# A two-layer conformer and sparse-attention stack: the layers' convolution in two stages, with the blocks' inputs made first and each block's sum over the taps a block later

## The chip, the cores and the metric

The kernel runs on one core of a Trainium2 chip. The metric is the device time of one execution in microseconds (us), the median of several runs. The engines are called as in the profile: PE (TensorE's matmuls) and PEld (its weight loads), DVE (VectorE), ACT (ScalarE), POOL (GpSimd) and SP (SyncE, which here only issues transfers). ACTq and SPq are the DMA issues of ACT and SP.

## The reference, cut to what matters

The program is a block of mixer, cross attention and mixture of experts, and then `second_block`, two layers of a convolution branch beside an attention branch. Only the layers are touched.

```python
for l in range(DEPTH_2):                       # 2 layers, x is 512 positions x 1024
    p = h @ w_in[l]                            # h: normalized, modulated x
    u_val, u_gate, g_conv, c_q, c_kv, k_idx, w_idx, g_attn = jnp.split(p, offsets, axis=-1)
    y_conv = conformer_conv(u_val, u_gate, ...) * jax.nn.silu(g_conv)
    y_attn = dsa_attention(c_q, c_kv, k_idx, w_idx, ...) * jax.nn.silu(g_attn)
    y = jnp.concatenate([y_conv, y_attn], axis=-1) @ w_out[l]
    x = x + gate[:, None, :] * rmsnorm(y, g_post[l])

def conformer_conv(u_val, u_gate, conv_w, conv_b, ln_g, ln_b, w_pw2):
    a = u_val * jax.nn.sigmoid(u_gate)
    y = <causal depthwise convolution of a, 31 taps, 512 channels> + conv_b
    return jax.nn.silu(layernorm(y, ln_g, ln_b)) @ w_pw2

def dsa_attention(...):
    score = jnp.einsum("bth,bths->bts", w_b, jax.nn.relu(s_raw))   # 8 index heads
    _, sel = lax.top_k(score, k_top)           # the 128 best keys of each query
    ...                                        # softmax attention over those keys, 8 heads
```

## The kernel before, in words

Values are kept as pairs of f16 (a high and a low part), so that each product is three matmuls (`mm3`: wh by hh, wh by hl, wl by hh). `mm` (L98, L99) records every matmul, so all PE rows have line 99 and are told apart by their tiles. `split` makes a pair: ACT writes the high part (L119), DVE the low part (L120). `load_w` does that for a block of weights: an SP transfer to `raw` (two buffers), then two halves of `wh` by ACT and of `wl` by DVE; four pairs of weights have buffers. `proj_feat` is the product of one block of weights, 256 columns in two halves, with the layer's input X (`hh`, `hl`): 24 matmuls of 128x512 for 128 features.

The order in which each engine takes its instructions is set by a scheduler at build time; `high_priority` moves instructions ahead and `after(x)` orders them behind x. In a layer the parts that matter here stand in this order in the code:

- `select` for query blocks 1, 2 and 3: for each of 8 index heads, PE makes scores (`at<-idx`, two banks of PSUM), ACT takes the positive part (`re`, L1583), DVE adds it into `sc` (L1586 for the first head, L1588 for the others). Then 16 rounds of MAX (L1592) and MATCH_REPLACE (L1593) on DVE take out the 128 best scores, and `msk` (L1595) marks them.
- `conv`, called twice for two blocks of 128 channels: the gate's projection into bank `cv`, a tanh on ACT (`cth`, L1650), the value's projection into a bank `mm`, the gating on DVE (L1653), the split into `cu` (L119, L120), and four DMAs issued by ACT (L1663) that copy `cu` into `R`, each with four shifted copies of 32 channels in 128 partitions. POOL builds the diagonal weights `wd` (L1669). Then 96 matmuls `po<-R,wd` sum over the taps (8 shifts by 3 parts by 4 groups) into the one bank `po`, and ACT moves it out with the bias (`cacc`, L1678). `R`, `cu` and `wd` have two buffers each.
- `conv_norm`: the layernorm; its mean is four f32 products `cv<-cacc,ones`, one for each block.
- twice: `gates` of the attention (projection into `cv`, ACT `gth` L1337, DVE `ga` L1339), two times `dsa` (two heads each: query projection `mm<-cq,uq`, scores `at<-kv,q` with the mask added by `at<-msk,identb`, softmax, transposes `tr`, value products `po<-pT,v`), then the convolution's gates and `conv_out`.
- `out_gain` builds the row `G` for the output: two ACT DMAs `gt<-in_r` (L1309), each followed by a POOL operation on `G` (L1310). `gt` shares its two buffers with `wd`.

The two lines that the split replaces in `layer` are

```python
for k in range(2):
    self.conv(pool, l, X, sp, cw, acc, k)
```

Of the kernel before, what the change touches and what calls it, by code (L numbers as in the profile page):

```python
# [12 lines left out]
F16 = mybir.dt.float16  # L13
BF16 = mybir.dt.bfloat16
I32 = mybir.dt.int32
AF = mybir.ActivationFunctionType
OP = mybir.AluOpType
# [3 lines left out]
P = 128  # L21
# [29 lines left out]
SA = 16.0  # L51
SW = 256.0
SX = 4.0
INV = 1.0 / (SA * SW)
# [9 lines left out]
class Kern:  # L64
# [43 lines left out]

    def mm3(self, out, L, R, start, stop):
        self.mm(out, L[0], R[0], start, False)  # L110
        self.mm(out, L[0], R[1], False, False)
        return self.mm(out, L[1], R[0], False, stop)

# [692 lines left out]
    def route_tile(self, low, pool, i, hf):  # L806
# [45 lines left out]

        R = sm("R8", NE)
        nc.vector.max(m8, LM)
        top = self.top[:, i]
        nc.vector.tensor_copy(top[:, 0:2], m8[:, 0:2])
        nc.vector.match_replace(R, top, LM, 3.0e38)
        Mh = self.Mh[:, i]
# [590 lines left out]
    def layer(self, pool, l, xin, follow):  # L1449
        nc, a = self.nc, self.a  # L1450
        sp, (X, cq, kv, widx, filled) = self.sp[l], xin[0]
        big = a["w2_big"]
# [36 lines left out]
        v = self.u8(pool, "v2").rearrange("p (h i f) -> p h i f", h=2, i=NT)  # L1489
# [6 lines left out]
        cw = pool.tile([P, 2, S], F16, name="cw2", tag="h", bufs=BUFS["h"])  # L1496
        self.split(sp[:, 24:152], cw[:, 0, :P], cw[:, 1, :P], SW)
        acc = pool.tile([P, 4, S], F32, name="cacc", tag="cacc", bufs=1)
        for k in range(2):
            self.conv(pool, l, X, sp, cw, acc, k)  # L1500
        z = self.conv_norm(pool, sp, acc)
        yh, yl = (pool.tile([P, 4, 1084], F16, name=n, tag="Y", bufs=2).rearrange("p g m -> p (g m)")[:, :DC * S]
                  .rearrange("p (c t) -> p c t", c=DC) for n in ("y2h", "y2l"))
# [3 lines left out]
            self.split(raw.rearrange("p (c f) -> p c f", c=4), wp[:, 0], wp[:, 1], SW)  # L1507
        wp = wp[:, 0], wp[:, 1]
        for k in range(2):
            gas = self.gates(pool, big[l, 8 + k], X)  # L1510
            for b in range(2):
                done = self.dsa(pool, gas[b], uq, cqh, cql, kvh, kvl, v[:, 0], v[:, 1], msk, yh, yl, 2 * k + b)
            gcs = self.gates(pool, big[l, 6 + k], X)
            for b in range(2):
                self.conv_out(pool, wp, z, gcs[b], 2 * k + b, yh, yl)

        G = self.out_gain(pool, l)
        ws = []
# [22 lines left out]
        for i in range(NT):  # L1541
            y = pool.tile([P, D], F32, name="yo", tag="yo", bufs=2)
            ss = pool.tile([P, 2], F32, name="oss", tag="oss", bufs=4)
            for hf in range(2):
                o = slice(hf * 512, (hf + 1) * 512)
                po = self.bank("mm")
# [13 lines left out]
            for hf in range(2):  # L1560
                o = slice(hf * S, (hf + 1) * S)
                nc.vector.scalar_tensor_tensor(self.x[i][:, o], y[:, o], r[:, 1:2], self.x[i][:, o],
                                               op0=OP.mult, op1=OP.add)
# [76 lines left out]
        nc.vector.tensor_tensor(ga, po, ga, OP.mult)  # L1640
        return self.split(ga, yh[:, 4 + hp], yl[:, 4 + hp], 0.5 * INV / 1024.0)

    def conv(self, pool, l, X, sp, cw, acc, k):

        nc, big = self.nc, self.a["w2_big"]
        wv, wg = self.load_w(big[l, 2 + k]), self.load_w(big[l, 4 + k])
        for b in range(2 * k, 2 * k + 2):
            pg = self.proj_feat(wg, X, 256, b % 2, out=self.bank("cv"))
            th = self.t2(pool, "cth", "v")
            nc.scalar.activation(th, pg, AF.Tanh, scale=0.5 * INV)  # L1650
            pu = self.proj_feat(wv, X, 256, b % 2)
            with self.tc.high_priority():
                nc.vector.scalar_tensor_tensor(th, th, 1.0, pu, op0=OP.add, op1=OP.mult)  # L1653

            u = pool.tile([P, 2, 544], F16, name="cu", tag="cu", bufs=2)
            nc.gpsimd.memset(u[:, :, 0:30], 0.0)
            nc.gpsimd.memset(u[:, :, 542:544], 0.0)
            with self.tc.high_priority():
                self.split(th, u[:, 0, 30:542], u[:, 1, 30:542], 0.5 * SA * INV)
            R = pool.tile([P, 4, 1084], F16, name="R", tag="Y", bufs=2)  # L1660
            for g in range(4):
                ug = u[32 * g:32 * g + 32]
                nc.scalar.dma_start(R[:, g], bass.AP(tensor=ug.tensor, offset=ug.offset,  # L1663
                                                   ap=[list(ug.ap[0]), [1, 4], [1, 1084]]))

            wd = pool.tile([P, 2, 32, 32], F16, name="wd", tag="yo", bufs=2)
            with self.after(self.lat_pow):
                for h in range(2):
                    nc.gpsimd.tensor_tensor(wd[:, h], self.mask4[:, None, :].to_broadcast([P, 32, 32]),  # L1669
                                            cw[:, h, 32 * b:32 * b + 32, None].to_broadcast([P, 32, 32]), OP.mult)  # L1670
            py = self.bank("po")
            for q in range(8):
                for n, (x, y) in enumerate(((0, 0), (0, 1), (1, 0))):
                    for g in range(4):
                        o = y * 544 + 4 * q
                        self.mm(py[32 * g:32 * g + 32], wd[:, x, 8 * g + q], R[:, g, o:o + S],
                                q + n == 0, q == 7 and n == 2)
            nc.scalar.activation(acc[:, b], py, AF.Identity, scale=INV, bias=sp[:, 152 + b:153 + b])  # L1678

    def conv_norm(self, pool, sp, acc):  # L1680

# [231 lines left out]
```

## Time and profile before

| | before |
|---|---|
| median of 3 runs | 1646.88 us (1646.11 to 1650.43) |
| the profiled execution, and its span | 1654.38 us, 1652.7 us |
| PE busy | 1511.4 us (91% of the span) |
| DVE busy | 973.2 us (59%) |
| ACT busy | 592.0 us (36%) |
| POOL busy | 113.7 us (7%) |

The span is cut from the first to the last recorded instruction of one profiled execution; the busy times are sums over it. PE is the engine with the most work, but the shares are means over stages with different limits.

### The profile page before, as it was taken

To read this page: it belongs to the slowest core of one execution; us is meant where nothing else is said; L and a number is where in the kernel's file an instruction comes from. 1 tells how busy PE (TensorE), PEld (TensorE's weight loads), DVE (VectorE), ACT (ScalarE), POOL (GpSimd) and SP (SyncE) were. 2 spreads that over 40 slices of the span, in tenths; PEclk is the share of its full clock that TensorE was granted. 3 is DMA by queue.
4 is the path that set the end of the run, shared out by engine and by line. 5 is a ranking of instruction groups with operands and counts; after the bars stand their busy time and mean duration, and the time that the engine had idled before them with its cause. 6 is when DMAs were issued, how large, how long until landed. Compare 5 with 4: busy or idle time off the path is not lost.

```text
span 1652.7 us, 25283 instructions
## 1 busy us (share of the span) xinstructions
PE 1511.4 (91%) x10208; PEld 828.4 (50%) x10208; DVE 973.2 (59%) x2076; ACT 592.0 (36%) x1230; POOL 113.7 (7%) x124
## 2 busy tenths in 40 slices
PE   7999999879996999999999987988999989888998
PEld 5344586765583444444444435323444863334457
DVE  5778848877754324233242447886746568947552
ACT  5355545423531101111011126522737454227461
POOL 0210001000000000000000021212000020110000
PEclk9999899999998999999999998989999999989999
DMA  8410223788457999999999940334011223230201
GB/s 284 157 62 12 91 82 111 290 255 328 147 224 283 385 426 427 427 426 427 426 426 426 426 154 14 109 105 131 10 68 43 75 96 100 67 121 26 77 26 52
DMA packets 55609, 323.03 MB, mean 195 GB/s; under 512 B 8720, under 2 KB 11584, under 8 KB 19520
## 3 DMA queue, kind: packets, MB, share of 16 engines
q1 hardware_dynamic: 45136, 306.01, 47.6%
q10 hardware_dynamic: 10352, 15.37, 3.5%
q8 instruction: 81, 1.33, 0.3%
q14 instruction: 40, 0.33, 0.1%
HBM read 310.35 MB, written 3.69 MB: 190 GB/s over the span
## 4 chain that ended last, share of the span: by engine, by line
PE 48%; DVE 9%; DMA 3%; ACT 3%; issue 2%; POOL 1%; ACTq 0%; DVEq 0%; POOLq 0%
PE h L99 12%; PE y L99 6%; PE mm L99 6%; PE cv L99 6%; PE po L99 4%; PE tr L99 4%; PE at L99 3%; PE ga L99 3%; DMA R<-cu 3%; DVE sc L1593 1%; DVE m L1592 1%; PE tr L1634 1%; DVE wl L120 1%; PE tr L103 1%; DVE sc L1588 1%
## 5 line engine op out<-in xcount | busy, mean ns | idle before, releaser
L99 PE MATMUL h<-raw,xg 128*64 128x512 f32 x1024 | 223.0, 593 | 0.0
L120 DVE SCALAR_TENSOR_TENSOR wl<-raw,wh 128x1024 f16<-128x1024 f32 (+1 forms) x107 | 133.3, 1251 | 63.6 <-ACT wh L119 63.0
L99 PEld LDWEIGHTS <-wh 128*128 128x128 f16 x1104 | 107.7, 100 | 124.2 <-issue 32.7
L99 PEld LDWEIGHTS h<-raw,xg 128*64 128x64 f32 x1024 | 73.5, 137 | 146.1 <-issue 145.7
L119 ACT ACTIVATE wh<-raw 128x1024 f16<-128x1024 f32 (+1 forms) x107 | 110.6, 1042 | 94.2 <-PE mm L99 43.4
L958 DVE SCALAR_TENSOR_TENSOR hm<-hm,h 128x512 f32<-128x512 f32 x16 | 11.0, 687 | 180.5 <-ACT hm L957 180.5
L99 PE MATMUL y<-raw,hT 128*64 128x512 f32 x512 | 113.6, 595 | 0.0
L987 DVE SCALAR_TENSOR_TENSOR x<-tr,x 128x512 f32<-128x512 f32 x128 | 86.4, 687 | 12.3 <-PE tr L99 10.3
L99 PEld LDWEIGHTS <-wl 128*128 128x128 f16 x552 | 54.9, 99 | 63.9 <-issue 14.4
L957 ACT ACTIVATE hm<-h 128x512 f32<-128x512 f32 x16 | 9.6, 597 | 207.2 <-PE h L99 182.8
L99 PEld LDWEIGHTS <-hh 128*128 128x128 f16 x768 | 74.7, 101 | 17.8 <-issue 3.7
L99 PE MATMUL po<-R,wd 128*32 128x512 f16 x768 | 56.9, 401 | 23.8 <-DMA R<-cu 23.8
L120 DVE SCALAR_TENSOR_TENSOR yl<-y,cw,yh 128x512 f16<-128x512 f32 x32 | 24.0, 750 | 89.1 <-ACT yh L119 89.1
L99 PE MATMUL cv<-hh,wh 128*128 128x512 f16 x192 | 74.8, 390 | 0.0
L99 PE MATMUL cv<-hl,wh 128*128 128x512 f16 x192 | 74.7, 389 | 0.0
L99 PE MATMUL cv<-hh,wl 128*128 128x512 f16 x192 | 74.7, 389 | 0.0
L99 PEld LDWEIGHTS <-hl 128*128 128x128 f16 x640 | 64.2, 100 | 14.0 <-issue 2.1
L99 PEld LDWEIGHTS y<-raw,hT 128*64 128x64 f32 x512 | 35.3, 137 | 70.3 <-issue 69.0
L99 PE MATMUL ga<-Sel,hl 128*128 128x128 f16 x480 | 67.8, 223 | 0.0
L99 PE MATMUL ga<-Sel,hh 128*128 128x128 f16 x480 | 67.8, 223 | 0.0
L1250 DVE CUSTOM_DVE_ANT_0 raw<-raw,cact 128x1024 f32<-128x1024 f32 x48 | 58.3, 1236 | 13.4 <-DMA raw<-in_w_ada 12.3
L119 ACT ACTIVATE yh<-y,cw 128x512 f16<-128x512 f32 x32 | 22.0, 687 | 114.2 <-PE y L99 112.9
(429 smaller groups left out, 3487.0 us busy)
## 6 DMA issues: line engine op xcount, KB each, us to landing
raw<-in_w_moe SPq DMA_DIRECT2D x192, 1024.0 KB, 12.1
raw<-in_w_pre SPq DMA_DIRECT2D x34, 1024.0 KB, 5.3
raw<-in_w_big SPq DMA_DIRECT2D x30, 1024.0 KB, 4.9
raw<-in_w_ada SPq DMA_DIRECT2D x24, 1024.0 KB, 6.6
R<-cu ACTq DMA_DIRECT2D x32, 271.0 KB, 5.2
x<-in_x_tm SPq DMA_DIRECT2D x4, 512.0 KB, 7.3
gt<-in_r ACTq DMA_DIRECT2D x4, 512.0 KB, 5.2
out<-x SPq DMA_DIRECT2D x4, 512.0 KB, 2.6
```

The source lines that it names most:

```text
L99: self.last_mm = self.pin(self.nc.tensor.matmul(out, lhsT, rhs, start=start, stop=stop, skip_group_check=True))
L103: return self.pin(self.nc.tensor.transpose(out, src, ident))
L119: return (nc.scalar.activation(hi, src, func, scale=scale), nc.vector.scalar_tensor_tensor(lo, src, scale, hi, op0=OP.mult, op1=OP.subtract))
L120: nc.vector.scalar_tensor_tensor(lo, src, scale, hi, op0=OP.mult, op1=OP.subtract))
L957: nc.scalar.activation(hm[:n], ph[0][:n], AF.Tanh, scale=0.5 / SA)
L958: nc.vector.scalar_tensor_tensor(hm[:n], hm[:n], 1.0, ph[0][:n], op0=OP.add, op1=OP.mult)
L987: self.last_add = nc.vector.scalar_tensor_tensor(xo, pc, 1.0 / 1024.0, xo, op0=OP.mult, op1=OP.add)
L1250: nc.vector.tensor_tensor_reduce(w, w, cact, 1.0, 0.0, OP.mult, OP.add, to)
L1588: nc.vector.scalar_tensor_tensor(sc, re[:, :W], s, sc, op0=OP.mult, op1=OP.add)
L1592: nc.vector.max(m8, sc)
L1593: nc.vector.match_replace(sc, m8, sc, -3.0e38)
L1634: nc.tensor.transpose(pt[:, (i - k) * P:(i - k + 1) * P], ps_[i][:, k * P:(k + 1) * P], self.ident)
```

## The change

`conv` becomes two functions. `conv_in` makes a block's input (projections, gating, split, the four shifted copies), and issues the copies alternately on ACT's and SP's queue. `conv_sum` builds `wd` and sums over the taps, its matmuls ordered behind the last matmul recorded before. The order is: inputs 0 and 1, the second pair of weights, sum 0, input 2, sum 1, input 3, the first `gates` of the attention (moved here from below the layernorm), sum 2, sum 3. Nothing is computed that was not computed before.

```diff
@@ layer
-        for k in range(2):
-            self.conv(pool, l, X, sp, cw, acc, k)
+        ws = [[self.load_w(big[l, n]) for n in (2, 4)]]
+        Rs = [self.conv_in(pool, X, *ws[0], b) for b in (0, 1)]
+        ws.append([self.load_w(big[l, n]) for n in (3, 5)])
+        gas = None
+        for b in range(4):
+            self.conv_sum(pool, sp, cw, acc, Rs[b], b)
+            if b < 2:
+                Rs.append(self.conv_in(pool, X, *ws[1], 2 + b))
+            if b == 1:
+                gas = self.gates(pool, big[l, 8], X)
...
         for k in range(2):
-            gas = self.gates(pool, big[l, 8 + k], X)
+            gas = gas or self.gates(pool, big[l, 8 + k], X)
...
-            gcs = self.gates(pool, big[l, 6 + k], X)
+            gas, gcs = None, self.gates(pool, big[l, 6 + k], X)
@@ conv_in
+            for g in range(4):
+                ug = u[32 * g:32 * g + 32]
+                (nc.scalar, nc.sync)[g % 2].dma_start(R[:, g], bass.AP(tensor=ug.tensor, offset=ug.offset,
+                                                                       ap=[list(ug.ap[0]), [1, 4], [1, 1084]]))
+        return R
@@ conv_sum
+        wd = pool.tile([P, 2, 32, 32], F16, name="wd", tag="yo", bufs=2)
+        with self.after(self.lat_pow):
+            ...
+        py = self.bank("po")
+        with self.after(self.last_mm):
+            for q in range(8):
+                ...
+        nc.scalar.activation(acc[:, b], py, AF.Identity, scale=INV, bias=sp[:, 152 + b:153 + b])
```

On PE, at the first sum of layer 0, the order before puts the first tap matmuls singly between matmuls of the next block's projection; each waits for one of the four copies (the DMAHW semaphores):

```order
L99 MATMUL cv<-hl_9249,wh 128x512
L99 LDWEIGHTS wd [waits Pool_49]
L99 MATMUL po<-R,wd 32x512 [waits DMAHW7_49]
L99 LDWEIGHTS wl
L99 MATMUL cv<-hh_9248,wl 128x512
L99 LDWEIGHTS wh
L99 MATMUL mm<-hh_9248,wh 128x512
```

In the order of the changed kernel both blocks' projections stand ahead, and the 96 matmuls follow each other:

```order
L99 MATMUL mm<-hl_9249,wh 128x512
L99 LDWEIGHTS wl
L99 MATMUL mm<-hh_9248,wl 128x512
L99 LDWEIGHTS wd [waits Pool_49]
L99 MATMUL po<-R,wd 32x512 [waits DMAHW7_49]
L99 LDWEIGHTS wd
L99 MATMUL po<-R,wd 32x512 [waits DMAHW0_49]
L99 LDWEIGHTS wd
L99 MATMUL po<-R,wd 32x512 [waits DMAHW1_49]
```

So the single tap matmuls and what stood between them have changed places: 48 matmuls of block 1's input now lie between the end of block 0's input and the first tap matmul. Sums 1, 2 and 3 stand whole in the same way; behind input 3 come the 24 matmuls of the first gate, 7 of the query projection, the 24 of the second gate, sum 2, and sum 3 one f32 product later.

On DVE, at the end of the rounds for query block 3 of layer 0 (`sc_10057`), the order before has block 3's gating behind the mask, and no gate:

```order
L1592 MAX m_10115<-sc_10057 128x8 [waits DVE_49]
L1593 MATCH_REPLACE sc_10057<-m_10115,sc_10057 128x512 [waits DVE_49]
L1595 TENSOR_SCALAR msk_10148<-sc_10057 128x512 [waits DVE_49]
L1653 SCALAR_TENSOR_TENSOR cth<-cth,mm 128x512 [waits PE_49]
L120 SCALAR_TENSOR_TENSOR cu<-cth,cu 128x512 [waits DMAHW4_49,DMAHW7_49,DMAHW0_49,Activation_49]
L120 SCALAR_TENSOR_TENSOR wl<-raw,wh 128x1024 [waits Activation_49]
```

In the order of the changed kernel (line numbers there are 7 or 8 higher) the gating, two halves of weights and the first gate stand among the last rounds:

```order
L1660 SCALAR_TENSOR_TENSOR cth<-cth,mm 128x512 [waits PE_49,Activation_49]
L1601 MATCH_REPLACE sc_10057<-m_10115,sc_10057 128x512 [waits DVE_49]
L1600 MAX m_10115<-sc_10057 128x8 [waits DVE_49]
L120 SCALAR_TENSOR_TENSOR cu<-cth,cu 128x512 [waits DMAHW6_49,DMAHW5_49,DMAHW7_49,DMAHW0_49,Activation_49]
L1601 MATCH_REPLACE sc_10057<-m_10115,sc_10057 128x512 [waits DVE_49]
L120 SCALAR_TENSOR_TENSOR wl<-raw,wh 128x1024 [waits DMAHW5_49,Activation_49]
L1600 MAX m_10115<-sc_10057 128x8 [waits DVE_49]
L120 SCALAR_TENSOR_TENSOR wl<-raw,wh 128x1024 [waits Activation_49]
L1339 SCALAR_TENSOR_TENSOR ga<-gth,cv 128x512 [waits Activation_49]
```

The first gate `ga` reads bank `cv`; the second gate's first matmul (`cv<-hh`, which waits for DVE) needs that bank, there is only one, and sums 2 and 3 stand behind it on PE. Between the last score addition and `ga` stand 14 and a half rounds, two `cth`, two `cu` and four `wl`.

On ACT, before, the move of sum 2 and the two `gt` transfers stand apart, with block 3's copies and two query splits between them:

```order
L1678 ACTIVATE cacc<-po,sp_3445 128x512 [waits PE_49]
L1309 DMA gt<-in_r 128x1024 [waits Pool_49]
L119 ACTIVATE cu<-cth 128x512 [waits DMAHW7_49,DMAHW0_49,DVE_49]
L119 ACTIVATE wh<-raw 128x1024 [waits PE_49]
L1663 DMA R<-cu 128x1x1084 [waits DVE_49,Pool_49]
L1663 DMA R<-cu 128x1x1084
L1663 DMA R<-cu 128x1x1084 [waits DMAHW2_49]
L119 ACTIVATE q_11022<-mm 128x512 [waits PE_49]
L1663 DMA R<-cu 128x1x1084 [waits DMAHW3_49]
L119 ACTIVATE q_11107<-mm 128x512 [waits PE_49]
L1309 DMA gt<-in_r 128x1024 [waits DMAHW6_49,DMAHW4_49,Pool_49]
```

The changed kernel has them together, the second gate's tanh ahead and the move of sum 3 right behind:

```order
L1337 ACTIVATE gth<-cv 128x512 [waits PE_49]
L1689 ACTIVATE cacc<-po,sp_3445 128x512 [waits PE_49]
L1309 DMA gt<-in_r 128x1024 [waits DMAHW4_49]
L1309 DMA gt<-in_r 128x1024 [waits DMAHW4_49,Pool_49]
L1689 ACTIVATE cacc<-po,sp_3445 128x512 [waits PE_49]
```

The second `gt` waits for POOL's addition of the first, so `cacc` of sum 3 now queues behind that transfer and that addition.

## Rows read from the trace of the kernel before

**Rows 1.** The page's chain of work that ended last, by line.

```profile
PE h L99 12%; PE y L99 6%; PE mm L99 6%; PE cv L99 6%; PE po L99 4%; PE tr L99 4%; PE at L99 3%; PE ga L99 3%; DMA R<-cu 3%; DVE sc L1593 1%; DVE m L1592 1%; PE tr L1634 1%; DVE wl L120 1%; PE tr L103 1%; DVE sc L1588 1%
```

**Rows 2.** Windows: stretch, us, busy PE PEld DVE ACT POOL, PEclk, DMA share, GB/s.

```profile
1065.80:1160.50 94.70, 81.67 (x599) 31.68 (x598) 70.32 (x163) 21.56 (x33) 13.97 (x14) 0.91 0.36 103
1160.50:1300.00 139.50, 134.35 (x773) 73.73 (x773) 86.36 (x186) 86.23 (x190) 2.10 (x3) 0.98 0.17 57
1386.60:1482.50 95.90, 79.62 (x599) 31.62 (x598) 70.21 (x162) 21.57 (x33) 13.48 (x10) 0.91 0.35 102
1482.50:1602.00 119.50, 114.81 (x599) 56.87 (x599) 72.20 (x161) 75.16 (x168) 1.02 (x1) 0.97 0.11 37
```

**Rows 3.** PE's waits, 1036 to 1245, then 1350 to 1600: total, times, longest.

```profile
PE po L99 <- DMA R<-cu: 10.2, 6, 3.0
...
PE po L99 <- DMA R<-cu: 13.6, 8, 3.0
```

**Rows 4.** PE's timeline in both layers' convolution: start, us, instruction [idle before].

```profile
1065.79 0.38 PE L99 MATMUL mm<-hh,wh 128*128 128x512 f16 x1
1070.97 0.38 PE L99 MATMUL cv<-hh,wh 128*128 128x512 f16 x1
1078.16 0.38 PE L99 MATMUL po<-R,wd 128*32 128x512 f16 x1 [2.06 <-DMA R<-cu]
1134.10 5.36 PE L99 MATMUL po<-R,wd 128*32 128x512 f16 x93
1140.69 2.74 PE L99 MATMUL cv<-cacc,ones 128*128 128x512 f32 x6
1147.65 0.38 PE L99 MATMUL at<-kv,q 128*128 128x128 f16 x3
1160.47 0.39 PE L99 MATMUL at<-msk,identb 128*128 128x512 bf16 x1
1482.47 0.39 PE L99 MATMUL at<-msk,identb 128*128 128x512 bf16 x1
```

**Rows 5.** DVE's waits, 1065.8 to 1122, then 1386.6 to 1442.

```profile
DVE sc L1588 <- ACT re L1583: 3.8, 2, 3.3
DVE wl L120 <- ACT wh L119: 3.0, 1, 3.0
...
DVE sc L1588 <- ACT re L1583: 2.9, 2, 2.4
DVE wl L120 <- ACT wh L119: 1.7, 1, 1.7
```

**Rows 6.** DVE's timeline, first and last score addition and first rounds of block 3.

```profile
1092.91 1.59 DVE L1586 TENSOR_SCALAR sc<-re,widx 128x512 f32<-128x512 f32 x1
1108.64 0.75 DVE L1588 SCALAR_TENSOR_TENSOR sc<-re,widx,sc 128x512 f32<-128x512 f32 x1 [3.26 <-ACT re L1583]
1109.90 0.69 DVE L1592 MAX8 m<-sc 128x8 f32<-128x512 f32 x1
1111.41 0.69 DVE L1592 MAX8 m<-sc 128x8 f32<-128x512 f32 x1
...
1413.72 0.46 DVE L1586 TENSOR_SCALAR sc<-re,widx 128x512 f32<-128x512 f32 x1
1427.40 0.75 DVE L1588 SCALAR_TENSOR_TENSOR sc<-re,widx,sc 128x512 f32<-128x512 f32 x1 [0.56 <-ACT re L1583]
```

**Rows 7.** DVE's weight splits, by line, 1065.8 to 1160.5: busy, mean ns, idle before.

```profile
L120 DVE SCALAR_TENSOR_TENSOR wl<-raw,wh 128x1024 f16<-128x1024 f32 x8 | 9.7, 1215 | 3.2 <-ACT wh L119 3.2
```

**Rows 8.** POOL's timeline: building a block's weights, adding to G.

```profile
1090.40 3.81 POOL L1669 TENSOR_TENSOR wd<-mask,cw 128x1024 f16<-128x1024 f16 x2 [7.96 <-PE po L99]
1143.34 3.31 POOL L1310 TENSOR_TENSOR G<-G,gt 128x1024 f32<-128x1024 f32 x1 [10.01 <-DMA gt<-in_r]
```

**Rows 9.** Time to landing of gt (1100 to 1500) and of raw (1340 to 1500).

```profile
DMA to landing us min/median/max: 3.7/5.2/8.2
...
DMA to landing us min/median/max: 4.8/5.0/9.6
```

More of the change, by code (lines that the diff above doesn't have):

```diff
@@ L1641, in dsa, with conv_in @@
         return self.split(ga, yh[:, 4 + hp], yl[:, 4 + hp], 0.5 * INV / 1024.0)
[L1643 to L1660, printed above, removed]
+    def conv_in(self, pool, X, wv, wg, b):
+        nc = self.nc
+        pg = self.proj_feat(wg, X, 256, b % 2, out=self.bank("cv"))
+        th = self.t2(pool, "cth", "v")
+        nc.scalar.activation(th, pg, AF.Tanh, scale=0.5 * INV)
+        pu = self.proj_feat(wv, X, 256, b % 2)
+        with self.tc.high_priority():
+            nc.vector.scalar_tensor_tensor(th, th, 1.0, pu, op0=OP.add, op1=OP.mult)
+        u = pool.tile([P, 2, 544], F16, name="cu", tag="cu", bufs=2)
+        nc.gpsimd.memset(u[:, :, 0:30], 0.0)
+        nc.gpsimd.memset(u[:, :, 542:544], 0.0)
+        R = pool.tile([P, 4, 1084], F16, name="R", tag="Y", bufs=2)
+        with self.tc.high_priority():
+            self.split(th, u[:, 0, 30:542], u[:, 1, 30:542], 0.5 * SA * INV)
@@ L1661, in conv @@
             for g in range(4):
                 ug = u[32 * g:32 * g + 32]
[L1663 to L1670, printed above, removed]
@@ L1671, in conv, with conv_sum @@
-            py = self.bank("po")
+                (nc.scalar, nc.sync)[g % 2].dma_start(R[:, g], bass.AP(tensor=ug.tensor, offset=ug.offset,
+                                                                       ap=[list(ug.ap[0]), [1, 4], [1, 1084]]))
+        return R
+    def conv_sum(self, pool, sp, cw, acc, R, b):
+        nc = self.nc
+        wd = pool.tile([P, 2, 32, 32], F16, name="wd", tag="yo", bufs=2)
+        with self.after(self.lat_pow):
+            for h in range(2):
+                nc.gpsimd.tensor_tensor(wd[:, h], self.mask4[:, None, :].to_broadcast([P, 32, 32]),
+                                        cw[:, h, 32 * b:32 * b + 32, None].to_broadcast([P, 32, 32]), OP.mult)
+        py = self.bank("po")
+        with self.after(self.last_mm):
@@ L1677, in conv @@
                                 q + n == 0, q == 7 and n == 2)
-            nc.scalar.activation(acc[:, b], py, AF.Identity, scale=INV, bias=sp[:, 152 + b:153 + b])
+        nc.scalar.activation(acc[:, b], py, AF.Identity, scale=INV, bias=sp[:, 152 + b:153 + b])
     def conv_norm(self, pool, sp, acc):
```

## The prediction

> **What bounds the kernel now.** I read the page's chain first: nearly all of it is PE, but one transfer stands on it, the copies `R<-cu`, with 3% of the span [rows 1]. The windows say where PE is not full. In the convolution of layer 0, 1065.8 to 1160.5, PE is busy 81.67 of 94.7 us, in layer 1 79.62 of 95.9; in the attention behind it 134.35 of 139.5 and 114.81 of 119.5 [rows 2]. So some 29 us are idle in the two stretches that the change rewrites, and the attention behind is bound by PE's work, with gaps of about 5 us in each layer. PE's waits name most of the idle time: the first tap matmuls wait for the copies, 10.2 us in layer 0 and 13.6 in layer 1 [rows 3]. Third I read DVE, which does the selection's rounds at the same time and works 70 of those 95 us [rows 2]: it is the engine that PE will wait for next.
>
> **The change part by part.** *The copies.* Before, block 0's input ends at 1070.97 and its first tap matmul waits at 1078.16; between them lies as much projection as the scheduler found [rows 4]. A projection of 24 matmuls takes 1070.97 − 1065.79 = 5.18 us, 0.216 each [rows 4]. After, 48 of them, 10.4 us, lie between block 0's input and its sum. That covers what lay between the end of the input and the first tap matmul before, 7.2 us, with 3.2 us to spare for the other three copies, and two queues issue two each. Blocks 1 to 3 have more work between. So I take the 23.8 us of waits for copies [rows 3] as gone. They don't enter the sum as such: what remains is to see what PE meets instead. For that I follow DVE.
>
> *DVE up to the first gate.* `gates` is moved ahead of sum 2, and its second half needs bank `cv`, which is free only after DVE's `ga` of the first half. On DVE `ga` stands behind 14 and a half rounds of block 3's selection. So PE's sum 2 now depends on when that selection started. Before, the last score addition of block 3 begins at 1108.64 in layer 0 and 1427.40 in layer 1 [rows 6]. Ahead of it DVE works the same instructions in both orders (two `cth`, two `cu`, four `wl` and the rounds of blocks 1 and 2). Its waits there are for `re` and for `wh`: 3.8 + 3.0 = 6.8 us in layer 0, 2.9 + 1.7 = 4.6 in layer 1 [rows 5]. I read both as PE or ACT being held behind the copies, and take them as gone: 1101.8 and 1422.8 (if they stay, 1108.6 and 1427.4, and that much of the gain goes). From there to the end of `ga`: 1.26 to the first round (1109.90 − 1108.64), 14 rounds of 1.51 (1111.41 − 1109.90) = 21.1, half a round 0.7 [rows 6], two `cth` and two `cu` 2.7 and `ga` 0.7 (0.7 each, a little under the 0.75 of the addition, the same kind on as much), four `wl` at 1.215 = 4.9 [rows 7]: 31.4. So `ga` ends at 1133.2 and 1454.2.
>
> *PE up to there.* PE is held at the fifth index score until about 1094, since that bank waits for DVE's first addition (1092.91 before, [rows 6]). Then: 33 matmuls of input 2, 7.1; four scores of three matmuls, 2.6; sum 1, 5.4 (5.36 for 93 [rows 4]); input 3, 10.4; the first gate, 5.2; six query matmuls, 1.3; and 2 for a stretch at half clock (the granted clock of the window is 0.91 [rows 2]). That is 34, PE is at the bank at about 1128, and waits 5 us. This is the new wait.
>
> *PE from there.* The second gate 5.2, with 1.7 for half clock after the wait; sum 2, 5.5; one f32 product of `cacc` 0.9 (2.74 for three, which the row counts as six [rows 4]); sum 3, 5.5: 18.8. Sum 3 ends at 1152.0 and 1473.0. Before, the row behind it starts at 1160.47 and 1482.47 [rows 4]: earlier by 8.5 and 9.5.
>
> *What PE has done by then.* More by the two gates, 48 × 0.216 = 10.4 us. Less by five or six query matmuls 1.1, two f32 products 1.8, and the first head's scores up to the last mask, 4480 columns at 0.216 us for 512, 1.9. Net 5.6 us more work done. The lead is 8.5 + 5.6 = 14.1 in layer 0, 15.1 in layer 1, together 29.2.
>
> *What is given back.* On ACT `cacc` of sum 3 queues behind the second `gt`, which waits for the first `gt` and POOL's addition. The first is issued when sum 2 ends, 1145.7; landing 5.2 [rows 9] and addition 3.3 [rows 8] give 1154.2, then `cacc` 0.8: 1155.0. PE has 1.8 us of other f32 products behind 1152.0, so it waits 1.2. By the landings of 3.7 and 8.2 [rows 9] it is 0 to 4.2. And the gates were cover in the attention: 10.4 us of PE work that could lie in any gap there no longer does. The gaps of the attention are 5.2 and 4.7 us [rows 2] with the cover; without it they could grow by 0 to 10.4 per layer. I take 1.5, near the low end, since other work of the same kind (the convolution's gates, `conv_out`, the second gates) stays there. Given back: 2 × (1.2 + 1.5) = 5.4.
>
> *Taken at nothing:* two of each block's four copies stand on SP's queue between weight transfers (`raw`), and a copy that waits there for its `cu` holds the transfers behind it. They land in 4.8 to 9.6 us [rows 9], and PE's other projections cover that as long as one block's (10.4 us) lies between; the price if not is rival B's. POOL builds the same `wd`, under PE's projections.
>
> *The sum.* −29.2 + 5.4 = −23.8 us. Profiled execution: 1654.4 → 1630.6. The runs' median is 7.5 us below that execution, so 1646.9 → **1623**.
>
> *A rule against the rows.* POOL's build of `wd` (1090.40, 3.81 us [rows 8]) lay under DVE's first addition of block 3, which took 1.59 us at 1092.91; in layer 1 the same instruction, without it, took 0.46 [rows 6]. The Trainium skill, page "SBUF — State Buffer", section "Who interferes with whom", says that DVE and GpSimd share a port pair, held by one for a whole instruction while the other is fully blocked. The row agrees in sign, not in size (1.1 us more, not the whole of POOL's instruction). In the new order `wd` is built earlier, right behind sum 0; by the rule DVE would be 1.1 us earlier per layer and the sum −26, about 1621. It is left out of the sum.
>
> **The rivals.** *B, a shallower gain.* The gates' weights now come in the middle of the convolution. If their `raw` lands in 9.6 us instead of 5.0, or the attention's cover is worth half of the 10.4, 5 us per layer go: −14, **1633**. For it: copies stand between weight transfers on SP's queue. Against it: the median landing is 5.0. *C, the full gain.* All of the 23.8 us of waits for copies and the half clock (0.09 of 95 us, 8.5 per layer [rows 2]) come back, with no new wait on `ga`: −41, **1606**. Against it: DVE works 70 of 95 us and its rounds can't be earlier than their scores. *D, no change.* All of the lead is given back in the attention, **1647**: it needs gaps there to grow by 15 us in each layer, more than the cover removed. *E, slower.* The first head's scores start at 1147.65 before [rows 4]; after, they stand behind sum 3 and three f32 products, at about 1155.9. If the attention ends by its own chain (scores, softmax, transposes, split, value product) and not by PE's work, each layer ends 8.2 us later: +16, **1663**. It decides from the point where PE's gaps in the attention exceed what it did ahead; against it, PE is busy 134.35 of 139.5 us there [rows 2].
>
> **How the numbers follow.** Mine 0.55, its own range 1614 to 1632 (the `gt` wait 0 to 4.2, the lost cover 0 to 5, the DVE waits gone wholly or half). B 0.20, C 0.12, D 0.05, E 0.08. The range for 8 in 10 takes in my case, B and the way down to C: 1606 to 1637. A change under 0.3%, about 5 us, could hardly be told from none: faster 0.87 (mine, B, C), same 0.05, slower 0.08.
>
> **What would show it.** Right: no waits of `po` for `R`; the rows of tap matmuls are 96 long; a wait of `cv` for DVE's `ga` of about 5 us per layer; a wait of `cv<-cacc` for ACT of 1 us; sum 3 ends some 9 us earlier in its layer. Wrong: a wait for `R` at sum 0 (10.4 us too little), a wait on `ga` well over 5 (then DVE's waits did not go), or an attention window with over 8 us of gaps.

## The result, and the profile after

The changed kernel takes 1629.53 us (median of 4 runs, 1626.61 to 1635.61) against 1648.5 for the kernel before (4 runs): a ratio of 0.9882, interval 0.986 to 0.9904, 19 us less. A second timing of the same file gave 1624.22 against 1650.27, 0.9846 (0.9829 to 0.9863). The profiled execution has a span of 1628.6 us, 24.1 less than the one of before; 3.1 of these lie ahead of the first layer's convolution, in code that did not change (the first index score starts at 1037.66 instead of 1040.78), so 21.0 belong to the layers: 4.7 in layer 0 and 16.3 in layer 1, where 11.4 and 12.4 were forecast.

PE's waits, layer 0 (1036 to 1245) and then layer 1 (1350 to 1600): total, times, longest. They answer to [rows 3]; only the lines that bear on the two stages are shown.

```profile
PE cv L99 <- DVE ga L1339: 6.0, 3, 4.5
PE at L99 <- ACT re L1591: 2.2, 1, 2.2
PE cv L99 <- ACT csq L1704: 2.1, 1, 2.1
PE po L99 <- DMA R<-cu: 0.8, 1, 0.8
...
PE cv L99 <- DVE ga L1339: 3.7, 2, 3.3
PE at L99 <- ACT re L1591: 3.6, 2, 3.1
PE cv L99 <- ACT cacc L1689: 1.6, 1, 1.6
```

The waits of the tap matmuls for their copies have gone from 10.2 + 13.6 to 0.8 us. In their place stand the wait of bank `cv` for DVE's gate, 4.5 and 3.3 us, and behind sum 3 a wait for `csq` (the squares of the layernorm) in layer 0 and for `cacc` in layer 1.

The page's chain by line no longer lists `R<-cu`, which stood there with 3% [rows 1]; the one transfer in the list is one of weights:

```profile
PE h L99 13%; PE y L99 7%; PE mm L99 6%; PE cv L99 5%; PE tr L99 4%; PE at L99 3%; PE ga L99 3%; PE po L99 3%; DVE sc L1601 2%; DVE m L1600 2%; DVE wl L120 2%; DMA raw<-in_w_big 2%; PE tr L1642 1%; PE tr L103 1%; DVE sc L1596 1%
```

Windows of the convolution and of the attention (columns as in [rows 2]), layer 0 and layer 1; each convolution starts as in [rows 2], earlier by what its layer begins earlier (3.1 and 7.8 us):

```profile
1062.70:1153.60 90.90, 82.30 (x628) 34.36 (x626) 71.86 (x165) 22.13 (x30) 11.57 (x13) 0.92 0.41 113
1153.60:1262.20 108.60, 104.79 (x540) 54.53 (x537) 65.17 (x159) 69.49 (x165) 3.38 (x2) 0.94 0.10 35
1378.80:1466.00 87.20, 80.83 (x623) 33.67 (x621) 69.38 (x159) 22.07 (x30) 7.91 (x9) 0.92 0.42 118
1466.00:1569.40 103.40, 99.12 (x537) 49.98 (x537) 64.95 (x157) 69.44 (x165) 6.18 (x3) 1.00 0.11 36
```

The attentions before, up to the same last value product:

```profile
1160.50:1271.60 111.10, 107.19 (x564) 53.37 (x564) 65.90 (x156) 70.27 (x162) 1.02 (x1) 0.97 0.12 39
1482.50:1594.40 111.90, 107.21 (x564) 53.42 (x564) 65.79 (x154) 70.26 (x162) 1.02 (x1) 0.97 0.11 38
```

The convolution is shorter by 3.8 and 8.7 us and holds 24 to 29 matmuls more; the attention is shorter by 2.5 and 8.5 us. The attentions do the same 537 to 540 matmuls, but one takes 108.6 us and the other 103.4: the granted clock was 0.94 in the first and 1.00 in the second. So about half of the difference between the layers comes from the convolution, whose idle time fell by 4.4 us in layer 0 and by 9.9 in layer 1 (windows less PE's busy time, against [rows 2]), and about half from the attention's clock.

PE's timeline, layer 0, from sum 0 on, then layer 1 from sum 3 on:

```profile
1079.37 0.40 PE L99 MATMUL po<-R,wd 128*32 128x512 f16 x3
1080.55 5.34 PE L99 MATMUL po<-R,wd 128*32 128x512 f16 x93 [0.78 <-DMA R<-cu]
...
1133.87 0.59 PE L99 MATMUL cv<-hh,wh 128*128 128x512 f16 x1 [4.51 <-DVE ga L1339]
1140.79 5.37 PE L99 MATMUL po<-R,wd 128*32 128x512 f16 x96
...
1148.27 5.36 PE L99 MATMUL po<-R,wd 128*32 128x512 f16 x96
1153.56 2.84 PE L99 MATMUL cv<-cacc,ones 128*128 128x512 f32 x6
...
1160.50 1.33 PE L99 MATMUL cv<-ones,csq 128*128 128x1 f32 x8 [2.09 <-ACT csq L1704]
...
1465.93 1.98 PE L99 MATMUL cv<-cacc,ones 128*128 128x512 f32 x4
1469.47 1.12 PE L99 MATMUL cv<-cacc,ones 128*128 128x512 f32 x2 [1.56 <-ACT cacc L1689]
```

DVE's timeline of layer 0, some rows from the first score addition of block 3 to the gate:

```profile
1090.34 0.46 DVE L1594 TENSOR_SCALAR sc<-re,widx 128x512 f32<-128x512 f32 x1
1099.11 0.75 DVE L1596 SCALAR_TENSOR_TENSOR sc<-re,widx,sc 128x512 f32<-128x512 f32 x1 [0.84 <-ACT re L1591]
1107.02 0.69 DVE L1660 SCALAR_TENSOR_TENSOR cth<-cth,mm 128x512 f32<-128x512 f32 x1 [3.66 <-PE mm L99]
1118.60 2.06 DVE L120 SCALAR_TENSOR_TENSOR wl<-raw,wh 128x1024 f16<-128x1024 f32 x1
1121.96 1.53 DVE L120 SCALAR_TENSOR_TENSOR wl<-raw,wh 128x1024 f16<-128x1024 f32 x1
1133.14 0.68 DVE L1339 SCALAR_TENSOR_TENSOR ga<-gth,cv 128x512 f32<-128x512 f32 x1
```

POOL's build of `wd` for sum 2:

```profile
1117.67 4.74 POOL L1679 TENSOR_TENSOR wd<-mask,cw 128x1024 f16<-128x1024 f16 x2
```

The last addition stands where the sum had it (1099.11 + 3.1 = 1102.2, forecast 1101.8). The gate is 3.7 us later than forecast, and DVE's wait at `cth` for PE's projection of input 2 alone is 3.66 us.

### The profile page after: what moved, and what is told of

Read it like the earlier page. It is cut to its first block, busy times and chain, and to the rows that moved or that the text cites. A ratio compares the mean times of both kernels' runs of the same rounds, so it can differ in the third digit from the quotient of the medians.

```text
span 1628.6 us, 25290 instructions
## 1 busy us (share of the span) xinstructions
PE 1506.8 (93%) x10208; PEld 831.3 (51%) x10208; DVE 971.6 (60%) x2076; ACT 592.2 (36%) x1230; POOL 112.9 (7%) x124
## 4 chain that ended last, share of the span: by engine, by line
PE 45%; DVE 13%; ACT 3%; issue 3%; DMA 2%; POOL 1%; DVEq 0%; POOLq 0%; ACTq 0%
PE h L99 13%; PE y L99 7%; PE mm L99 6%; PE cv L99 5%; PE tr L99 4%; PE at L99 3%; PE ga L99 3%; PE po L99 3%; DVE sc L1601 2%; DVE m L1600 2%; DVE wl L120 2%; DMA raw<-in_w_big 2%; PE tr L1642 1%; PE tr L103 1%; DVE sc L1596 1%
## 5 line engine op out<-in xcount | busy, mean ns | idle before, releaser
L1250 DVE CUSTOM_DVE_ANT_0 raw<-raw,cact 128x1024 f32<-128x1024 f32 x48 | 58.2, 1234 | 11.6 <-DMA raw<-in_w_ada 10.7
L152 POOL TENSOR_TENSOR rs_r<-rs_t,mhalf 128x1 f32<-128x1 f32 (+1 forms) x34 | 25.1, 742 | 432.9 <-DVE rs_t L151 432.9
```

Of the source, the lines that this page charges most:

```text
L152: self.last_pow = nc.gpsimd.tensor_tensor(r[:, :n], t[:, :n], self.mhalf[:, :n], OP.pow)
L1250: nc.vector.tensor_tensor_reduce(w, w, cact, 1.0, 0.0, OP.mult, OP.add, to)
```

## The experiments

Each is the changed kernel with the edit shown, unless the text says otherwise. The last column is made from the list of executions: the span of each times its mean granted clock, and of these the median. It is an estimate of what the span would be with the clock at 2.4 GHz throughout (half of the time at 1.2 GHz taken off); PE is not at work in all of that time, so it holds to a few us.

| kernel | median, us | ratio to before (95%) | span x clock, us |
|---|---|---|---|
| before (beside these runs) | 1648.9 to 1651.9 | 1 | 1591 to 1593 |
| changed, first timing | 1629.53 | 0.9882 (0.986 to 0.9904) | 1573 |
| changed_again | 1624.22 | 0.9846 (0.9829 to 0.9863) | 1572 |
| one_queue | 1625.01 | 0.9853 (0.9833 to 0.9873) | 1573 |
| gates_late | 1637.06 | 0.9928 (0.9906 to 0.995) | 1573 |
| stages_only | 1638.87 | 0.9933 (0.9909 to 0.9957) | 1572 |
| two_queues | 1652.38 | 1.001 (0.9993 to 1.0026) | 1590 |
| second_bank | 1626.05 | 0.986 (0.9836 to 0.9884) | 1571 |
| half_rounds | 1625.92 | 0.9851 (0.9824 to 0.9877) | 1573 |
| bank_free | 1626.62 | 0.9863 (0.9837 to 0.9889) | 1570 |
| ln_fill | 1622.35 | 0.9845 (0.9819 to 0.9872) | 1574 |
| busy_gap | 1618.26 | 0.982 (0.9798 to 0.9842) | 1578 |
| busy_elsewhere | 1637.08 | 0.9921 (0.9891 to 0.995) | 1581 |
| gap_gate | 1613.51 | 0.9781 (0.9751 to 0.981) | 1567 |

**changed_again**, no edit.

> The changed kernel once more, unedited, so that the edits of this call can be read against it on the same chip. Expected: 16 to 22 us under the kernel before, PE's wait for the first gate's bank 4.5 us in layer 0 and 3.3 in layer 1 as in its first profile, and the half-clock spell of 13.7 us at the head of layer 0's attention if the wait for csq comes again.

1624.22 us. The wait on the gate's bank is there again (4.9 and 3.3 us), the wait for `csq` in layer 0 is not, and neither attention has a stretch at half clock: the profiled span is 1618.0 at a mean clock of 0.972, against 1628.6 at 0.965 in the first profile. Times the clock both are 1572 to 1573.

**one_queue**, **two_queues**, **gates_late**, **stages_only** take the change apart.

```diff
-  (nc.scalar, nc.sync)[g % 2].dma_start(R[:, g], ...)      # one_queue, stages_only
+  nc.scalar.dma_start(R[:, g], ...)
-  if b == 1:                                               # gates_late, stages_only
-      gas = self.gates(pool, big[l, 8], X)
```

two_queues is the kernel before with the first pair of lines the other way round.

> The changed kernel with all four copies of a block issued by ACT. Theory (the two stages give the copies 10.4 us of projection as cover, the queue matters little): 0 to 3 us slower than the changed kernel, a wait of the first sum for the copies of 1 to 2 us per layer. Rival (two queues are what removed the waits): waits for the copies of 4 us or more per layer, 8 us or more slower.

> The kernel before with its copies issued alternately by ACT and SP, and nothing else changed. Theory (what removed the waits is the other block's projection between input and sum): the first copies land as late as before, the later ones somewhat earlier, waits for the copies fall from 23.8 us to 14 or more, the time by 0 to 8 us. Rival (the queues removed them): waits under 8 us, 16 us or more faster.

> The changed kernel with the attention's first gates back below the layernorm. Theory (DVE's rounds pace sums 2 and 3 whatever stands between): the wait on the gate's bank goes, sum 3 waits some 7 us for block 3's copies instead, sum 3 ends about 12 us earlier with 11.9 us less PE work done, so the time is that of the changed kernel within 4 us. Rival (the gates are the work that filled the waits): 10 us per layer slower, about the time of the kernel before.

> The two stages alone: the order of inputs and sums of the changed kernel, all copies on ACT's queue, the attention's gates where they were. From the runs so far (gates moved back 13 us slower by the medians, one queue 1 us): 1637 to 1643 us, with a wait of sum 3 for the copies of 7 to 10 us per layer. If the stages were worth nothing without the gates: 1650 us, as the kernel before.

One queue costs nothing that can be told (1625.0 beside 1624.2); PE waits for no copy there, but 3.8 us in each layer for a query split that stands behind four copies on ACT. Two queues gain the kernel before nothing (1.001). Its waits for copies did not even fall, as both theories had it, but rose from 23.8 to 32.2 us. SP issued its copies within 0.1 us of ACT's in each block of layer 0, here in input 1:

```profile
1095.78 1.19 SPq L1663 DMA_DIRECT2D R<-cu  x2
1095.75 1.90 ACTq L1663 DMA_DIRECT2D R<-cu  x2
```

But from issue to landing the copies took 7.3 us in the median, where they took 5.2 in the kernel before; why is not shown. So the second queue has no part in the result. The stages alone give 1638.9, 10 us under the kernel before, and the gates' move 13 us more; that is neither the 4 us at most of the theory of gates_late nor the 20 us of its rival. But by the last column the stages alone are already at 1572, 20 us under the kernel before, and the gates' move adds nothing: what it adds in time is clock. In stages_only PE's waits for copies were 3.7 and 4.4 us, less than expected; 5.0 and 4.0 us more went to waits for ACT to free the bank `po`. The wait that the gates' move covers is the one that gates_late shows ahead of sum 3, here in layer 0, where the 96 matmuls behind it then take 7.49 instead of 5.36 us:

```profile
1129.29 7.49 PE L99 MATMUL po<-R,wd 128*32 128x512 f16 x96 [7.37 <-DMA R<-cu]
```

**second_bank**: the second half of the early gates needs no `ga`.

```diff
-  self.proj_feat(w, X, 256, b, out=self.bank("cv"))
+  self.proj_feat(w, X, 256, b, out=self.bank("tr" if b and early else "cv"))
```

> The changed kernel with the second half of the early gates in one of the two banks that the transposes use later, so that it need not wait for DVE's gate of the first half. Theory (the wait on the bank is a real loss of PE time): sum 3 ends 7 to 9 us earlier in its layer and the time falls by 13 us against the changed kernel (6 to 18). Rival (DVE's chain is the bound and the wait only moves on, to the layernorm's products or the first head's softmax): within 3 us of the changed kernel, with a new wait of some 5 us per layer behind sum 3.

The rival holds in time (1626.1), though the wait moved to a place that neither named: PE's sum 3 waits 6.48 us in layer 0 for ACT to move sum 2 out of the one bank `po`, and ACT has the split of the next gates' weights ahead of that, whose transfer is late. PE's row:

```profile
1145.53 7.20 PE L99 MATMUL po<-R,wd 128*32 128x512 f16 x96 [6.48 <-ACT cacc L1689]
```

ACT's timeline ahead of it:

```profile
1142.90 1.06 ACT L119 ACTIVATE wh<-raw 128x1024 f16<-128x1024 f32 x1 [9.57 <-DMA raw<-in_w_big]
1144.81 0.67 ACT L1689 ACTIVATE cacc<-po,sp 128x512 f32<-128x512 f32 x1
```

**half_rounds** takes DVE's work away: it leaves out half of the selection of query block 3.

```diff
-  for k in range(KTOP // 8):
+  for k in range(KTOP // (16 if i == 3 else 8)):
```

> The changed kernel with 8 instead of 16 rounds of the selection for query block 3 (half of that block's keys are not selected, so part of the computation is left out), 12 us less of DVE's work per layer ahead of the first gate. Theory (DVE's rounds set when the gate's bank is free and what follows): the wait on the gate's bank goes and the time falls by 8 to 14 us, to 1610 to 1616. Rival (the wait only moves on, to the weights of the next gates and ACT's queue, as in the run with the second bank): within 3 us of 1624.

1625.9: the rival. The waits on `ga` fall to 2.2 and 0.8 us at the longest, and others come (two of 1.3 us for `nm` of the softmax, in each layer). DVE's rounds set where PE waits, not how long the layer takes.

**bank_free** keeps second_bank's edit and removes its new wait, by two edits on ACT's queue (the code is abbreviated).

```diff
-  w = self.load_w(src)                       # the convolution's first gates
+  raw = self.raw_w(src)
+  with self.after(cacc_of_sum_3):
+      w = self.load_w(None, raw=raw)
-  nc.scalar.dma_start(gt, ...)
+  nc.sync.dma_start(gt, ...)
```

> The second gate in a bank of the transposes, as before, and two edits on ACT's queue: the split of the convolution gates' weights is ordered behind the move of sum 3, and the gt transfers are issued by SP. Theory (with the second bank the wait moved to ACT, whose move of sum 2 stood behind a weight split that waited for its transfer: 6.5 and 3.8 us): those waits go and the time falls to 1612 to 1618. Rival (DVE's chain through the selection, layernorm and softmax is the bound): 1622 to 1627, with a new wait of PE on DVE or on csq.

The edits did what they say: from the index scores in input 2 up to the layernorm PE waits for nothing, and in layer 0 sum 3 ends at 1137.7 instead of 1149.1 in changed_again, 9.5 us earlier when the 1.9 us by which the layer began earlier are taken off. And yet the median is 1626.6. The profiled execution is the fastest of the six (1615.5; the others took 1624.0 to 1630.5 at lower clocks, and no trace shows where those lost it), but even in it the lead is gone at the end of the attention, which takes 114.0 us from the end of sum 3 to the last value product, where changed_again takes 102.6 in layer 0. What takes the lead begins behind sum 3 in PE's timeline:

```profile
1137.62 2.84 PE L99 MATMUL cv<-cacc,ones 128*128 128x512 f32 x6
1140.30 2.32 PE L99 MATMUL mm<-cq,uq 128*128 128x512 f16 x10
...
1145.25 1.05 PE L99 MATMUL cv<-ones,csq 128*128 128x1 f32 x8 [2.08 <-ACT csq L1707]
```

The windows there (17.5 us, then the rest of the attention of layer 0; the same stretch of layer 1):

```profile
1142.80:1160.30 17.50, 14.99 (x66) 10.91 (x65) 9.19 (x20) 6.91 (x14) 2.21 (x2) 0.61 0.16 59
1160.30:1251.70 91.40, 87.91 (x461) 41.77 (x462) 57.67 (x143) 63.35 (x153) 0.00 (x0) 1.00 0.14 47
1446.50:1464.10 17.60, 15.04 (x66) 10.98 (x65) 9.29 (x20) 7.00 (x14) 2.22 (x2) 0.61 0.16 58
```

PE waits 2.1 us for the layernorm's squares, and from just behind that wait on the granted clock is at 1.2 GHz: 0.61 over 17.5 us is 13.7 us at half clock, 6.8 us of work lost in each layer. That is the larger part of the 11.4 us; 10 matmuls that changed_again had done earlier are some 2 us, and PE's gaps are 2.3 us longer.

What makes the wait is on DVE and POOL. DVE subtracts the mean from four blocks (`cacc<-cacc,cmu`), ACT squares them. In bank_free's layer 0 the first subtraction begins while POOL is at its second operation on `G`, and takes 2.84 us instead of 0.68; in ln_fill (below) no operation on `G` lies there, and all four take 0.68. POOL's row and DVE's subtractions (min/median/max in ns) in bank_free, then those in ln_fill:

```profile
1141.16 2.83 POOL L1310 TENSOR_TENSOR G<-G,gt 128x1024 f32<-128x1024 f32 x1 [3.66 <-DMA gt<-in_r]
L1705 DVE TENSOR_TENSOR cacc<-cacc,cmu x4: 674/678/2840, 1141.7 to 1146.3; 128x512 f32<-128x512 f32 x4
L1712 DVE TENSOR_TENSOR cacc<-cacc,cmu x4: 676/677/678, 1155.9 to 1157.7; 128x512 f32<-128x512 f32 x4
```

In every layer with a wait for `csq`, one subtraction took 1.7 to 2.85 us and lay under that operation; where none was stretched so, in the kernel before, two_queues, second_bank, ln_fill and gap_gate, PE did not wait for `csq`. No run moves POOL's operation alone. The next runs ask whether it is the wait that the half clock follows.

**busy_gap**, **busy_elsewhere**, and **ln_fill** and **gap_gate** with useful work.

```diff
+  pd = self.bank("tr")          # busy_gap: between the mean and the squares
+  for k in range(28):           # busy_elsewhere: ahead of sum 2
+      self.mm(pd, X[0][:, k % 8, :P], X[0][:, k % 8], k == 0, k == 27)
...
+  pg = self.proj_feat(w6, X, 256, 0, out=self.bank("tr"))   # gap_gate: between mean and squares
...
+  self.gate(pool, pg, gc)                                   # gap_gate: behind the squares
```

The first three stand on bank_free; gap_gate takes over its bank and its `gt` on SP, but loads the convolution gates' weights right behind the early gates, without the order behind sum 3, and has a third buffer for the gates. ln_fill moves the second half of the early gate into the same place.

> The kernel of bank_free with 28 matmuls of 128x512 added between the layernorm's mean and its squares in each layer; their result is read by nothing, so they are 6.0 us of extra PE work per layer. Theory (in bank_free the wait for csq, 2.1 us in each layer, is what the 13.7 us at half clock behind it follow): with PE at work through it the wait goes and so do both spells; 8.9 us back and 6.0 us of extra work per layer, so 0 to 6 us faster than bank_free although PE does 12 us more, and the profiled span less half of the slow time 6 to 9 us longer than in bank_free. Rival (the clock falls for the one-column products and the small scores there, wait or no wait): the spells stay, 8 to 12 us slower than bank_free.

> A control for busy_gap: the same 28 added matmuls per layer, read by nothing, but ahead of sum 2 instead of in the wait for csq. Theory (it is the wait that the clock answers to): the wait for csq of 2 us and the spells behind it stay as in bank_free, and the added work is paid in full: 8 to 14 us slower than bank_free, 1634 to 1641. Rival (more matmuls anywhere keep the clock up): no spells in the attention, within 3 us of busy_gap's 1618.

> The kernel of bank_free with the second half of the early gate moved from ahead of sum 2 to between the layernorm's mean and its squares, so that useful work of 5.2 us lies in the wait for csq. Theory (that wait and the half clock behind it are what took the gain of bank_free back): the waits for csq and the spells of 13.7 us go, a wait for the copies of 1 to 3 us comes ahead of sum 3, and the time falls to 1612 to 1620. Rival (the attention's own chain sets its end, whatever PE has done ahead): within 3 us of bank_free's and the changed kernel's 1624 to 1627.

> The kernel of bank_free with useful work in place of the 28 added matmuls of busy_gap: the first half of the convolution's gates (24 matmuls, 5.2 us), whose weights are now loaded right behind the attention's gates, stands between the layernorm's mean and its squares; its tanh and product come behind the squares, and a third buffer holds the result. Theory (the wait for csq and the half clock behind it cost bank_free its gain): no wait for csq, no spell of 13.7 us there, and 12 us less PE work than in busy_gap: 1606 to 1614. Rival (the attention's chain sets the end, and busy_gap was fast for another reason): 1618 to 1627.

busy_gap does 12 us of work for nothing and is 8 us faster than bank_free by the medians, 7 by the ratios to before; DVE's stretched subtraction is there (2.85 us), but no wait for `csq` and no half clock in either attention. By the profiled executions, from the first index score to the end, the two take the same, 578.0 and 578.1 us, with the 12 us of added work in one. busy_elsewhere does the same work ahead of sum 2: the wait for `csq` is there (2.06 us), the half clock behind it too, and the time is 10 us over bank_free. So the gain comes from where the matmuls lie, not from their number. Whether PE's wait itself counts or the dense work that now lies ahead of the small products is not separated by these runs. gap_gate puts work there that had to be done anyway, and is the fastest of all: 1613.51, 38 us under the kernel before. In it DVE's subtractions are not stretched beyond 1.0 us either, since POOL's second operation on `G` came later; so its gain over bank_free, 13 us by the medians but 2.3 by the profiled executions, can't be put down to the filled wait alone. The same 17.5 us behind the layernorm's mean, in busy_gap (layers 0 and 1), busy_elsewhere (layer 0) and gap_gate (layers 0 and 1):

```profile
1145.30:1162.80 17.50, 16.51 (x104) 10.25 (x102) 12.17 (x25) 8.39 (x16) 2.19 (x2) 1.00 0.31 114
1451.60:1469.10 17.50, 16.51 (x104) 10.25 (x103) 12.16 (x25) 9.01 (x17) 2.28 (x2) 1.00 0.35 121
```

```profile
1148.60:1166.10 17.50, 15.13 (x73) 10.61 (x72) 9.40 (x21) 7.47 (x15) 2.27 (x2) 0.71 0.18 61
```

```profile
1146.60:1164.10 17.50, 16.54 (x104) 10.48 (x104) 9.36 (x26) 7.84 (x17) 3.37 (x2) 1.00 0.08 29
1451.70:1469.20 17.50, 16.55 (x104) 10.48 (x104) 9.04 (x25) 7.58 (x16) 3.79 (x2) 1.00 0.00 2
```

104 matmuls instead of 66 or 73 go through PE in the same time. ln_fill is between (1622.4, above its theory's 1612 to 1620): its gate is gone from ahead of sum 2, and sum 3 waits again for its copies (2.63 us in layer 0, the 94 matmuls behind it 7.66 us), so one gap is filled by opening another.

## Why the prediction was right

The forecast was −23.8 us, 1623; measured were −19 and −26, 1629.5 and 1624.2. The parts came out less well than the sum. Sum 3 ended 3.8 and 8.7 us earlier in its layer in the first profile, 8.1 and 7.4 in changed_again, where 8.5 and 9.5 were forecast. Up to the last value product, counted from each layer's first index score, the layers are shorter by 6.3 and 17.2 us in the first profile and by 16.5 and 16.4 in the second, where 11.4 and 12.4 were forecast. What differs between the two is mainly how much half clock fell into the layer, which the forecast did not foresee; that the first sum came out within 5 us is in part luck.

- **The copies**: right. 48 matmuls of projection cover them, 23.8 us of waits became 0.8 (1.6 in changed_again), and one queue would have done.
- **DVE up to the gate**: right to a microsecond at the last score addition of layer 0, where the waits ahead of it went for the most part; in layer 1 those for `re` stayed (3.6 us, before 2.9), the addition came 1.6 us late and the gate's end 0.8. Missing in the sum is that DVE in turn waits for PE at `cth` (3.66 us in layer 0). PE was late there because it had waited 2.2 us for ACT to free a bank of scores and then ran 10.2 us at half clock (a window from 1092.9 to 1103.1 has a granted clock of 0.50). In changed_again that stretch had the full clock, DVE waited for nothing there, and the gate's end, set back by the 3.4 us by which that layer began earlier, is 1132.7 (forecast 1133.2).
- **The new wait on `ga`**: 4.5 and 3.3 us for a forecast of 5. As a mechanism it stands, as a price it does not: with the bank given (second_bank) or DVE's work taken away (half_rounds) the time stayed. The 5 us per layer were not there to be had by either edit alone.
- **`cacc` behind `gt`**: in layer 1 ACT issues the two transfers over 9.06 us and PE waits 1.6 (forecast 1.2); in layer 0 ACT's move was not late, and the price shows one step later, at `csq`, 2.1, through POOL's operation on `G` that follows the second `gt`.
- **The lost cover in the attention**: forecast 1.5 us per layer. PE's gaps in the two attentions are 3.8 and 4.3 us (108.60 − 104.79, 103.40 − 99.12), before 3.9 and 4.7 up to the same last value product: nothing was lost there. What moved by much more is the clock: 13.7 us at half in layer 0's attention of the first profile, 6.8 us of time, and none in layer 1's. The sum had half clock only in the convolution (2 and 1.7 us); in the attention that term was missing, and it is a little over half of the 11.6 us between the layers.
- **The rule on the shared port**: the first addition fell from 1.59 to 0.46 us, but two weight splits then fell into POOL's next build and took 2.06 and 1.53 instead of 1.22. The contention moved, so there was no gain. But it was not nothing: the change also brought POOL's second operation on `G`, which before lay ahead of the layernorm, under DVE's subtraction, which took 2.72 us in layer 0 instead of 0.68 and made the wait for `csq`. The Trainium skill (page "SBUF — State Buffer", section "Who interferes with whom") calls the port pair that the two engines share an exclusive lock. The trace agrees in size too: POOL's operation ended at 1159.24 and the subtraction, begun at 1157.07, at 1159.79. The prediction read its own row as too short for that rule, 1.1 us more under a build of 3.81; but the addition began at 1092.91, and the build ended at 1094.21, 1.3 us later, so a full block could not have added much more.
- **The rivals**: B's late weights exist, but hidden until second_bank laid them open. D and E, the attention giving the lead back, did not happen to the changed kernel. Something like it did happen to bank_free, for the larger part by the clock.

What remains open is what decides how much half clock follows a wait. Behind a wait for `csq` of 1.9 to 2.1 us it was 13.7 us in layer 0 of the first profile, in both layers of bank_free and in layer 1 of gates_late, and 10.2 in both layers of busy_elsewhere (3.4 more came later in layer 1): six of six. In the other 18 layers of the kernels with two stages, where that wait was 1.5 us or less or none, the attention had none in 11 (layer 1 of changed_again among them, with the 1.5), 3.4 us in four, 6.8 in two, and 10.2 in layer 1 of stages_only, without any wait for `csq`. And the wait of 2.2 us for a bank of scores was followed by 10.2 us in the first profile and by none in changed_again.

## What to carry to other kernels

A wait of PE can cost more than its length: look at the granted clock of the stretch behind it, and compare variants by the span times the clock before you explain a difference between them. When a copy is covered by moving work, ask which gap that work had been filling; here a good place for 24 matmuls was the layernorm's gap of two microseconds. And ask what makes a gap before you fill it: this one came from POOL and DVE at work at the same time. An issue split over two queues was worth nothing here, with the cover and without it.

## What was not expected of the hardware

A short wait was dear: in bank_free PE worked nearly without a break up to the layernorm, waited 2.1 us, and was granted 1.2 GHz for 13.7 us, in both layers. 6.0 us of useless matmuls in that wait kept the clock at 2.4 GHz over the same stretch and paid for themselves (1618.3 against 1626.6 us). One DVE operation of 0.68 us took 2.84 while POOL worked on `G`, and with it began that wait. The Trainium skill, page "TensorE: Matmul & The Clock Gate", section "HAM oscillation — how this bites in real kernels", tells of a kernel whose every wait for a transfer sends the clock down again; these runs agree in part: six waits of 1.9 to 2.1 us on ACT were followed by a fall, and the wait of 2.2 us in changed_again was not. Eight versions whose medians lie between 1622 and 1639 us agree within 4 us, 1570 to 1574, when their spans are multiplied by their clocks.
